# Second block's query, key, gate and pool columns by seven block products instead of eight

## The chip, the cores and the metric

The kernel runs on one core of one Trainium2 chip. The metric is the device time of one execution in microseconds (us). Matrix products run on TensorE ("PE" in the profile; "PEld" is its weight load). VectorE ("DVE") and ScalarE ("ACT") do the elementwise work, GpSimd ("POOL") issues the accumulating transfers, SyncE ("SP") issues most of the others. Each engine works through its own list of instructions in order, and waits on semaphores for the others.

## The reference

One layer of a decoder for 2048 tokens of width 1024, in float32:

```python
h = rmsnorm(x, mix_norm_g)
proj = h @ w_in                                  # 1024 x 2560
q, k, v, g, u = split(proj, 512 columns each)
y_ret  = silu(g) * head_rmsnorm(retention(rope(q), rope(k), v))   # 4 heads of 128
y_pool = pool_mixer(u, pool_w) * pool_scale      # 4 groups of 128, windows 2, 4, 8, 16
x = x + concat(y_ret, y_pool) @ w_out
x = x + cross_attn(rmsnorm(x), rmsnorm(mem))     # 4 heads, 256 memory tokens
x = x + conv_glu_ffn(rmsnorm(x))                 # 1024 -> 2 x 2816 -> 1024, causal width-3 convolution
return rmsnorm(x)
```

The change is in `h @ w_in` for the second half of the tokens. Of its 20 groups of 128 columns, 16 are touched: four query, four key, four gate and four pool groups. The four value groups are not.

## The kernel before

**Tiling.** Tokens stand along the free dimension, features along the 128 partitions. The tokens are two blocks of 1024 (`T`), each of two halves of 512 (`SUB`); the 1024 features are eight groups `k` of 128. Every float32 operand is split into a high and a low part: `hi = round(x)` on ACT, `lo = x - hi` on DVE (`split`, or `high` and `low`). A product is three matmuls, high x high, high x low, low x high (`passes`, L241 to L243), each 128x128 by 128x512. The parts of weights go through three slots of the tile Q, raw weights through five slots of the tile R.

**The stage around the change**, for each block: `values` makes v (192 matmuls). `head_inputs` makes gate, query and key of one head by `unit`: one group of 128 columns, two PSUM banks (one for each 512 tokens), 48 matmuls over k, then `evac`. For query and key that is the rotary embedding straight from PSUM on DVE. `pool_group` does the same for a pool group, then window sums on DVE. `retention` of a head is a generator: `unit` advances it once per 12 matmuls (`next(behind[0])`), so that a head's attention runs beside the next head's projections. It works on two halves `a` and `c` of four chunks each. `scores` (L740, transposed keys L742), `states` (L751, then three chained steps on DVE), `values` (L764, L766), squares on ACT (L770), a reciprocal root of some 12 tiny DVE operations, `mixed` (transposes L779, gate, split). Block 1 starts with pool groups 3 and 2, then values, heads 0 to 3, pool groups 0 and 1, and then the output projection, which reads all eight results `mix[k]` as split tiles from `B`.

**Seven products already stand in the MLP.** There weights of two column groups are combined beforehand by transfers (`weight_sums`, L906: four copies from SP and four accumulating ones from POOL for each pair, spread over the first stages by `next(under[0])`), tiles are combined by `sums_of`, and `run` works through seven block products of 12 matmuls per pair (`Member`, `gathered`): products 0, 2, 4 and 6 pile up in one bank, 1 and 5 in a second, 3 has a third, and after each product `evac` copies or adds the bank's present content.

**Order.** The program's order gives priorities; a scheduler in the compiler then sets the order on each engine. What it chose is quoted below where it matters.

## Time and profile before

| | |
|---|---|
| median of 3 runs | 2475.38 us (2471.82 to 2476.74) |
| the profiled execution | 2470.94 us, its span 2469.2 us |
| PE busy | 2430.5 us, 98% of the span |
| DVE busy | 1706.8 us, 69% |
| ACT busy | 1219.9 us, 49% |
| POOL busy | 182.9 us, 7% |
| TensorE clock, mean | 0.996 |

Matmuls are pipelined and the profile models their ends: a record reads 0.39 us though the next matmul starts about 0.23 us later. How fast PE goes is therefore read from the count of matmuls in a window, not from its busy share. DVE's and ACT's records overlap a little as well. A wait is time in which an engine sat idle before an instruction, with the instruction that released it.

### The profile page before, as it was taken

What the parts mean: (1) busy time and instruction counts of PE and PEld (TensorE: products, weight loads), DVE (VectorE), ACT (ScalarE), POOL (GpSimd) and SP (SyncE); (2) the same over time, 40 slices, a digit from 0 to 9 for tenths busy, and PEclk for the clock granted to TensorE, in tenths of its full rate; (3) what the DMA queues carried; (4) which work ended last, traced back from release to release, by engine and by line L of the source; (5) the groups of instructions that cost most, each with busy time, mean ns of one, the idle gap of its engine ahead of it and who ended that gap; (6) DMA issues with size and microseconds to landing.
All of it is one profiled execution on the core that took longest, in us unless ns stands there. A gap on an engine that the chain in (4) does not pass through costs nothing.

```text
span 2469.2 us, 33010 instructions
## 1 busy us (share of the span) xinstructions
PE 2430.5 (98%) x11390; PEld 2032.3 (82%) x11390; DVE 1706.8 (69%) x2913; ACT 1219.9 (49%) x2170; POOL 182.9 (7%) x240
## 2 busy tenths in 40 slices
PE   6999999999999999999999999999999999999997
PEld 6888888888888888888888888888888888888886
DVE  8646576564636574575679776896767688867875
ACT  6333423443421223434655555665555577666663
POOL 1010121100021110000000100020000000000000
PEclk9999999999999999999999999999999999999998
DMA  9363889726676674366568655765457479768951
GB/s 321 91 167 116 233 198 246 230 49 196 189 189 154 152 160 147 111 223 223 156 205 275 208 182 156 229 211 174 154 158 217 135 228 309 238 189 281 345 169 68
DMA packets 257176, 474.27 MB, mean 192 GB/s; under 512 B 26864, under 2 KB 56176, under 8 KB 257008
## 3 DMA queue, kind: packets, MB, share of 16 engines
q1 hardware_dynamic: 212912, 409.23, 50.7%
q0 software_dynamic: 19584, 34.61, 9.2%
q10 hardware_dynamic: 24512, 28.32, 3.3%
q8 instruction: 89, 1.46, 0.2%
q14 instruction: 79, 0.65, 0.1%
HBM read 370.87 MB, written 170.39 MB: 219 GB/s over the span
## 4 chain that ended last, share of the span: by engine, by line
PE 95%; DVE 2%; DMA 1%; ACT 1%; issue 0%; POOLq 0%; POOL 0%; SPq 0%; ACTq 0%; DVEq 0%
PE mm L241 30%; PE mm L243 30%; PE mm L242 30%; PE aux L751 1%; PE aux L852 1%; PE aux L764 1%; PE aux L740 1%; PE aux L766 1%; PE aux L243 1%; PE aux L242 1%; PE aux L241 1%; PE aux L317 1%; DVE Z L216 0%; DMA R<-wo 0%; DMA Z<-xT 0%
## 5 line engine op out<-in xcount | busy, mean ns | idle before, releaser
L241 PE MATMUL mm<-G,Q 128*128 128x512 f32 (+1 forms) x1888 | 726.2, 385 | 17.2 <-ACT Q L233 11.3
L243 PE MATMUL mm<-G,Q 128*128 128x512 f32 (+1 forms) x1888 | 724.7, 385 | 4.6 <-DVE Q L216 4.4
L242 PE MATMUL mm<-G,Q 128*128 128x512 f32 (+1 forms) x1888 | 723.8, 384 | 0.0
L242 PE MATMUL mm<-G 128*128 128x512 f32 (+1 forms) x1380 | 530.0, 384 | 0.0
L241 PE MATMUL mm<-G 128*128 128x512 f32 (+1 forms) x1380 | 528.3, 385 | 0.4 <-ACT T L474 0.4
L243 PE MATMUL mm<-G 128*128 128x512 f32 (+1 forms) x1380 | 528.2, 385 | 0.0
L241 PEld LDWEIGHTS mm<-G,Q 128*128 128x128 f32 x1888 | 357.0, 189 | 85.8 <-ACT Q L233 11.9
L243 PEld LDWEIGHTS mm<-G,Q 128*128 128x128 f32 x1888 | 356.6, 189 | 73.7 <-DVE Q L216 5.7
L242 PEld LDWEIGHTS mm<-G,Q 128*128 128x128 f32 x1888 | 357.0, 189 | 67.9 <-DVE G L216 0.4
L241 PEld LDWEIGHTS mm<-G 128*128 128x128 f32 x1380 | 259.3, 188 | 51.9 <-ACT T L474 0.6
L242 PEld LDWEIGHTS mm<-G 128*128 128x128 f32 x1380 | 259.3, 188 | 51.4
L243 PEld LDWEIGHTS mm<-G 128*128 128x128 f32 x1380 | 259.3, 188 | 51.3
L1008 ACT ACTIVATE G<-R 128x512 fp32r<-128x512 f32 (+1 forms) x272 | 167.2, 616 | 251.9 <-PE mm L242 243.4
L216 DVE TENSOR_TENSOR Q<-R,Q 128x512 fp32r<-128x512 f32 x235 | 162.5, 694 | 151.3 <-ACT Q L233 136.8
L216 DVE TENSOR_TENSOR Z<-Z,mm 128x512 f32<-128x512 f32 x284 | 193.9, 683 | 101.8 <-PE mm L243 101.6
L225 DVE SCALAR_TENSOR_TENSOR Z<-Z,vecs 128x1024 f32<-128x1024 f32 x176 | 224.7, 1281 | 50.4 <-ACT Z L1071 45.8
L216 DVE TENSOR_TENSOR G<-R,G 128x512 fp32r<-128x512 f32 (+1 forms) x268 | 178.6, 675 | 109.7 <-ACT G L1008 70.7
L233 ACT ACTIVATE Q<-R 128x512 fp32r<-128x512 f32 x150 | 93.6, 628 | 243.1 <-PE mm L242 221.4
L1008 ACT ACTIVATE Q<-R 128x512 fp32r<-128x512 f32 (+1 forms) x204 | 125.5, 615 | 98.0 <-PE mm L242 80.6
L216 DVE TENSOR_TENSOR G<-T,G 128x512 fp32r<-128x512 f32 (+1 forms) x201 | 133.0, 677 | 45.0 <-ACT G L957 31.0
L216 DVE TENSOR_TENSOR T<-T 128x512 f32<-128x512 f32 (+3 forms) x218 | 149.3, 689 | 18.0 <-ACT T L357 9.7
L1071 ACT ACTIVATE Z<-Z,vecs 128x1024 f32<-128x1024 f32 x88 | 109.1, 1241 | 33.0 <-DVE Z L216 32.1
(216 smaller groups left out, 2480.9 us busy)
## 6 DMA issues: line engine op xcount, KB each, us to landing
R<-Ud SPq DMA_DIRECT2D x176, 256.0 KB, 2.8
T<-Gd SPq DMA_DIRECT2D x168, 256.0 KB, 4.4
R<-w_up SPq DMA_DIRECT2D x132, 256.0 KB, 3.2
Gd<-Z SPq DMA_DIRECT2D x110, 256.0 KB, 2.8
Ud<-w_up SPq DMA_DIRECT2D x88, 256.0 KB, 6.3
R<-w_qkgu SPq DMA_DIRECT2D x32, 512.0 KB, 4.5
R<-Dd SPq DMA_DIRECT2D x64, 256.0 KB, 4.4
Gd<-T SPq DMA_DIRECT2D x56, 256.0 KB, 3.5
```

The costliest lines, as they stand in the source:

```text
L216: return eng.tensor_tensor(out=out, in0=a, in1=b, op=op)
L225: dve.scalar_tensor_tensor(out=out, in0=a, scalar=s, in1=b, op0=op0, op1=op1)
L233: act.activation(hi, src, AF.Copy)
L241: pe.matmul(ps, lh, rh, start=start, stop=False, skip_group_check=more)
L242: pe.matmul(ps, lh, rl, start=False, stop=False, skip_group_check=more)
L243: latest[0] = pe.matmul(ps, ll, rh, start=False, stop=stop, skip_group_check=more)
L317: pe.matmul(ps[:, t : t + 1], ap, one, start=True, stop=more is None)
L740: pe.matmul(col(sc, c), self.ch(k, c), self.ch(q, c), start=True, stop=True)
L751: pe.matmul(col(self.kv, c), col(self.kn.f, c), self.ch(v, c, h * T), start=True, stop=True)
L764: pe.matmul(col(y, c), col(self.pr.f, c), self.ch(v, c, h * T), start=True, stop=self.cur[c] is None)
L1008: act.activation(p2[:, 0, :w], self.raw[i].f[:, :w], AF.Copy)
L1071: act.activation(self.c[g].f, a[:, 2:], AF.Identity, bias=cb[:, f : f + 1], scale=cw[2][:, f : f + 1])
```

## The change

For block 1 alone, the 16 groups of 128 columns become eight pairs, worked through in the order of `PAIRS`. Numbers 0 to 3 are queries, 4 to 7 keys, 8 to 11 gates, 12 to 15 pool groups. A pair is a 2x2 block product (two column groups, two halves of the features, two halves of the tokens) done by seven products of 12 matmuls.

- The weights' sums go to `Ad` in DRAM by eight more jobs of `weight_sums`, ahead of the MLP's. `quarter_sums` reads x of the block again (16 transfers) and makes the token side's sums; three of the seven operands are new tiles (t1, t2, t3), the others stand in X.
- `values` now comes first, its weights loaded during the last unit of block 0's attention.
- `head_projections` runs 56 products. `evac` copies or adds, and `final` scales a finished quarter. A query's or key's rotary embedding takes two half copies on ACT into one shared scratch (`side`) and three DVE operations.
- Retention leaves its result unsplit (`out` is None) and scales y on ACT, four instructions a half, in place of one on DVE. Pool groups are summed in steps beside the products (`pool_steps`). The results are split only when the last pair is under way or done (`settle`), since t1 to t3 occupy their places until then. Pool group 0's result goes to the tile E, which is free only when head 3's result is split.
- Places: `B` is 12 slots of G and four of E, raw weights get 3 + 2 slots of R and S, the split weights five places during the stage.

```diff
+PAIRS = ((15, 8), (0, 4), (14, 9), (1, 5), (10, 11), (2, 6), (3, 7), (12, 13))
...
-    def values(rn, wp):
+    def values(rn, wp, step=lambda: None):
...
+                    step()
...
-                tt(dve, four(self.kn.f[:, :SUB]), four(y), bcast(rr, P), ALU.mult)
+                if out is not None:
+                    tt(dve, four(self.kn.f[:, :SUB]), four(y), bcast(rr, P), ALU.mult)
+                else:
+                    for c in range(4):
+                        act.activation(col(self.kn.f, c), col(y, c), AF.Identity, scale=rr[:, c : c + 1])
...
-        jobs = [((w_up[f], w_up[f + NF]), 0, 4, Ud[f]) for f in range(NF)]
+        jobs = [((w_qkgu[a], w_qkgu[c]), 0, 4, Ad[p]) for p, (a, c) in enumerate(PAIRS)]
+        jobs += [((w_up[f], w_up[f + NF]), 0, 4, Ud[f]) for f in range(NF)]
...
+    def quarter_sums(b, t1, t2, z3, z4):
+        for j in range(KT // 2):
+            x = [TT.take() for _ in range(4)]
+            for i, r in enumerate(x):
+                k, at = j + 4 * (i // 2), b * T + i % 2 * SUB
+                sp.dma_start(r.f[:, :SUB], xT[k * P : (k + 1) * P, at : at + SUB])
...
+            act.activation(t, x12, AF.Identity, scale=g1)
+            tt(dve, x12, x11, x12, ALU.subtract)
+            split(x12, *fourth(t1, j), g1)
...
+            stt(d3, x22, g2, t, ALU.mult, ALU.subtract)
+            stt(x11, x11, g1, d3, ALU.mult, ALU.add)
+            negated(x11, *fourth(t2, j))
...
+            stt(d4, x21, g2, x11, ALU.mult, ALU.subtract)
...
+    def head_projections(b, v, rb, tabs, t1, t2, z3, z4):
...
+            def evac(self, i, ps):
+                role, q = ((0, 0), (1, 1), (0, 1), (0, 0), (1, 1), (0, 1), (1, 0))[i]
+                d = self.acc[role][q]
+                if (role, q) == (1, 0):
+                    self.final(role, q, d, ps)
+                elif (role, q) in self.seen:
+                    tt(dve, d, d, ps, ALU.subtract if role else ALU.add)
+                    self.final(role, q, d, d)
+                else:
+                    self.seen.add((role, q))
+                    act.activation(d, ps, AF.Copy, scale=-1.0 if role else 1.0)
...
+                if kind < 2:
+                    cs, cols = tables[0], slice(q * SUB, (q + 1) * SUB)
+                    c, sn = cs.f[:, cols], cs.f[:, T + q * SUB : T + (q + 1) * SUB]
+                    for to, at in ((slice(0, 64), slice(64, 128)), (slice(64, 128), slice(0, 64))):
+                        act.activation(side[to], src[at], AF.Copy, scale=1.0 if src is d else -1.0)
+                    tt(dve, side, side, sn, ALU.mult)
+                    times(d, src, c)
+                    tt(dve, d, d, side, ALU.add)
...
+        items = [(m, i) for m in members for i in (range(7) if m is members[0] else (0, 2, 4, 6, 1, 3, 5))]
...
+        for at, (m, i) in enumerate(items):
...
+            for j in range(KT // 2):
+                passes(ps, [pr[:, h, j * P : (j + 1) * P] for h in range(2)], operand(i, j), j == 0 and i in (0, 1, 3), j == KT // 2 - 1, i != 3)
+            made[at].free()
+            m.evac(i, ps)
+            fill()
+            next(behind[0], None)
+            step()
+            step()
+            next(under[0], None)
+            if m is members[-1]:
+                if i in (1, 2, 4):
+                    (t1, t2, t3)[(1, 2, 4).index(i)].free()
+                if at >= len(items) - 6:
+                    settle()
+                    settle()
+            if at % 7 == 6 and m.groups[0] < 4:
+                finish()
+                behind[0] = kept(m.groups[0])
...
+        finish()
+        while todo:
+            step()
+        while ready:
+            settle(True)
...
+            v = values(lambda: normed[0], wv, between)
...
+            mix, S = head_projections(b, v, rb, tabs, t1, t2, z3, z4)
...
+            if n == KT - 1 and b + 1 < NB:
+                finish()
+                wv = []
+                behind[0] = opening(prob[0][0], wv)
```

In the rows below, `mm_...` is a PSUM bank of products and `aux_...` one of retention's. First PE at the end of the stage. Before, the second half of head 3 has its values (L766, L764) here, and its transposes (L779) stand further down:

```order
L766 MATMUL aux_6895<-T,Z_4498 128x128
L764 MATMUL aux_6895<-Z_4498,T 128x128
L766 MATMUL aux_6895<-T,Z_4498 128x128
L241 MATMUL mm_6874<-G,Q 128x512
L242 MATMUL mm_6874<-G,Q 128x512
L243 MATMUL mm_6874<-G,Q 128x512
```

Then, 51 matmuls after those values, in the output projection, PE has before:

```order
L243 MATMUL mm_7079<-G,Q 128x512
L779 MATMUL aux_6956<-consts,T 128x128 x4
L241 MATMUL mm_7079<-G,Q 128x512
L242 MATMUL mm_7079<-G,Q 128x512
L243 MATMUL mm_7079<-G,Q 128x512
```

Of the changed kernel, PE at the same place; the values are L790 and L792, the transposes L809, first for the first half (`aux_7037`), then for the second (`aux_7124`):

```order
L792 MATMUL aux_7043<-T,E_5473 128x128
L790 MATMUL aux_7043<-Z_4501,T 128x128
L792 MATMUL aux_7043<-T,E_5473 128x128
L809 MATMUL aux_7037<-consts,T 128x128 x4
L267 MATMUL mm_7166<-G,Q 128x512
L267 MATMUL mm_7240<-G,Q 128x512
L268 MATMUL mm_7166<-G,Q 128x512
L269 MATMUL mm_7166<-G,Q 128x512
L268 MATMUL mm_7240<-G,Q 128x512
L269 MATMUL mm_7240<-G,Q 128x512
L267 MATMUL mm_7167<-G,Q 128x512
L809 MATMUL aux_7124<-consts,T 128x128 x3
```

Between the second half's values and its transposes stand seven matmuls, where there were 51.

Second, PE where a bank is written on. Before, a unit fills its two banks in turn, and PE passes from one to the other:

```order
L242 MATMUL mm_5701<-G,Q 128x512
L243 MATMUL mm_5701<-G,Q 128x512
L241 MATMUL mm_5702<-G,Q 128x512
L242 MATMUL mm_5702<-G,Q 128x512
L243 MATMUL mm_5702<-G,Q 128x512
```

In the changed kernel, PE in the pair of query 0 and key 0, at the end of product 4 and the start of product 6:

```order
L268 MATMUL mm_5655<-G,S_5474 128x512
L269 MATMUL mm_5655<-G,S_5474 128x512
L267 MATMUL mm_5806<-G,S_5474 128x512
L268 MATMUL mm_5806<-G,S_5474 128x512
L267 MATMUL mm_5655<-G,Q 128x512
L268 MATMUL mm_5655<-G,Q 128x512
```

Product 6 adds to the bank that ACT has to copy after product 4, with two matmuls between; pairs (1, 5) and (2, 6) have the same distance, elsewhere it is five matmuls or more.

Third, DVE at a query's rotary embedding. Before, it reads the bank:

```order
L216 TENSOR_TENSOR Z_4498<-mm_5701,Z_4498 128x512
L216 TENSOR_TENSOR T<-mm_5701,Z_4498 64x512 x2
L216 TENSOR_TENSOR Z_4498<-Z_4498,T 128x512
L216 TENSOR_TENSOR Z_4498<-mm_5702,Z_4498 128x512
L216 TENSOR_TENSOR T<-mm_5702,Z_4498 64x512 x2
```

In the changed kernel, DVE in the pair of query 0 and key 0:

```order
L242 TENSOR_TENSOR Z_4501<-Z_4501,mm_5740 128x512
L242 TENSOR_TENSOR R<-R,Z_4501 128x512
L242 TENSOR_TENSOR Z_4501<-Z_4501 128x512
L242 TENSOR_TENSOR S_5474<-R,S_5474 128x512
L242 TENSOR_TENSOR Z_4501<-Z_4501,R 128x512
L242 TENSOR_TENSOR Q<-R,Q 128x512
L242 TENSOR_TENSOR R<-R,Z_4501 128x512
```

The second row works on the scratch that ACT has to fill after the first row; the fourth and sixth are the low parts of weights for products still to come, and stand behind it.

More of the change, by code (lines that the diff above doesn't have):

```diff
@@ L93, in free, with __init__, take @@
             assert self.first + j not in self.arena.freed
-            self.arena.freed[self.first + j] = self.arena.clock
-            self.arena.clock += 1
+            self.arena.freed[self.first + j] = Arena.tick()
         if self.back is not None:
             self.back()
+class Joined:
+    def __init__(self, *arenas):
+        self.arenas = list(arenas)
+    def take(self, n=1):
+        fits = [(a.oldest(n), at) for at, a in enumerate(self.arenas) if a.oldest(n) is not None]
+        assert fits, "no room"
+        return self.arenas[min(fits)[1]].take(n)
 class Places:
@@ L827, in attention @@
         scl, nscl = (smp.tile([P, 8], F32, tag="scl", name=nm("scl"), bufs=2) for _ in range(2))
-        room = B.take(2 * KT)
-        third = [Region(B, room.first + KT * i, KT) for i in range(2)] + [new_z(F32R).take(KT)]
-        prob = [third[1], third[0]]
+        low, high, far = B.arenas[0].take(KT), B.arenas[0].take(KT // 2), B.arenas[1].take(KT // 2)
+        tables = [low, None, new_z(F32R).take(KT)]
+        prob = [([high, far], [high.r, far.r]), ([low], [low.r[:, : 4 * T], low.r[:, 4 * T :]])]
         def load_m(hp):
@@ L1532, in trunk, with between @@
     for b in range(NB):
-        early = (3, 2) if b else ()
-        pooled = {g: pool_group(b, g, normed[1]) for g in early}
-        finish()
-        rn, rb, last = normed
-        assert rn is not None and rb
-        if b:
+        if b == 0:
+            rn, rb, last = normed
+            v = values(lambda: rn, wv)
+            with tc.issue_after(last.ins):
+                tabs = list(rope_tables(0))[-1]
+            cs = rope_scale(tabs, rb)
+            per = [(0, 1, 1), (0, 1, 1), (0, 2, 2), (0, 2, 3)]
+            mix = []
+            for h in range(HEADS):
+                qkg = head_inputs(h, rb, cs, lambda i: folded(per[h][i]))
+                mix.append(B.take(2))
+                behind[0] = retention(b, h, qkg, v, mix[h])
+            folded(100)
+            pooled = {g: pool_group(b, g, rb) for g in (0, 3, 2, 1)}
+            finish()
+            cs.free()
+            mix += [pooled[g] for g in range(4)]
+            mix = [(u, [u.r[:, :T], u.r[:, T:]]) for u in mix]
+        else:
+            t1, t2 = (B.arenas[0].take(4) for _ in range(2))
+            z3, z4 = Z.take(2), Z.take(2)
+            more_sums = quarter_sums(b, t1, t2, z3, z4)
+            def between():
+                next(behind[0], None)
+                if next(more_sums, None) is None:
+                    next(under[0], None)
+            v = values(lambda: normed[0], wv, between)
+            for _ in more_sums:
+                pass
+            finish()
+            rb = normed[1]
             tabs = [TT.take() for _ in range(2)]
@@ L1596, in trunk, with opening @@
         acc = []
+        def opening(room, wv):
+            yield
+            for r in room:
+                r.free()
+            for kp in range(KT // 2):
+                wv.append(value_weights(kp))
+                if kp:
+                    yield
         def fetch_acc(n):
```

271 lines of the change are left out of this document (217 added, 54 removed).

## The prediction

> **What bounds the kernel now.** I read the chain that ended last first, then PE's waits over the whole program, then the same waits in the stage of the change (640 to 960 us, block 1 from its first projections into the output projection), then busy time by windows: the stage, and two stretches of the MLP, which already works by seven products. First from the page:
>
> ```profile
> PE 95%; DVE 2%; DMA 1%; ACT 1%; issue 0%; POOLq 0%; POOL 0%; SPq 0%; ACTq 0%; DVEq 0%
> ```
>
> PE's waits of the whole program, the two largest:
>
> ```profile
> PE mm L241 <- ACT Q L233: 11.3, 4, 9.1
> PE mm L241 <- DVE T L216: 4.7, 1, 4.7
> ```
>
> And all that PE waits for from 640 to 960 us:
>
> ```profile
> PE mm L241 <- ACT G L233: 0.9, 1, 0.9
> ```
>
> PE carries the end, and in this stage it waits 0.9 us in all. So a matmul removed here is time removed, as long as no new wait comes; and any new wait is time added.
>
> ```profile
> core 0: us, PE busy (x) PEld busy (x) DVE busy (x) ACT busy (x) POOL busy (x), PEclk, DMA share, GB/s
> 658.00:912.00 254.00, 254.00 (x1295) 215.88 (x1294) 154.66 (x351) 56.57 (x140) 50.42 (x62) 1.00 0.72 168
> ...
> 1300.00:1350.00 50.00, 50.00 (x223) 41.40 (x222) 47.08 (x64) 28.19 (x43) 4.26 (x6) 1.00 0.83 280
> 1350.00:1400.00 50.00, 50.00 (x222) 41.44 (x221) 38.39 (x49) 28.52 (x43) 5.59 (x6) 1.00 0.68 214
> ```
>
> The stage takes 254 us, DVE is busy 61% of it, ACT 22%. A saturated PE runs 222 matmuls in 50 us: 0.2252 us each. In the first MLP window DVE is busy 94% and PE still runs 223; a full DVE alone does not stall PE.
>
> **What the change removes.** Eight pairs of 2x2 blocks take 8 x 7 x 12 = 672 matmuls in place of 8 x 8 x 12 = 768. Retention's and the later stages' matmuls keep their numbers. 96 x 0.2252 = **21.6 us less** of PE.
>
> **What it adds, and where it hides.** Counted over both orders, DVE gets 88 more operations of 128x512 and 32 fewer of 64x512; ACT gets 69 more of 128x512, 32 of 64x512, 32 of 128x128; POOL 32 more accumulating transfers; SP 104 more transfers of 256 KB and 16 fewer of 512 KB.
>
> ```profile
> L216 DVE TENSOR_TENSOR T<-mm,Z 64x512 f32<-64x512 f32 x64 | 44.0, 688 | 1.1
> L216 DVE TENSOR_TENSOR Z<-mm,Z 128x512 f32<-128x512 f32 x32 | 22.0, 687 | 14.8 <-PE mm L243 14.6
> L1054 ACT ACTIVATE Z<-mm 128x512 f32<-128x512 f32 x176 | 102.2, 581 | 3.2 <-PE mm L243 2.7 <-DVE Z L225 0.5
> L920 POOL DMA_DIRECT2D Ud<-w_up x22 | 25.1, 1159 | 7.0 <-DMA Ud<-w_up 6.5 <-issue 0.2
> ```
>
> Half the partitions cost DVE as much as all, so it is 56 more operations at 0.687: 38.5 us, and DVE goes from 154.7 to 193.2 of the remaining 232 us, 83%. ACT: 101 x 0.58 + 32 x 0.28 (the 128x128 rows below) = 67.5 us, 56.6 to 124, 53%. Both stay under the 94% that the MLP window carries with no loss of PE: at nothing, so far as only totals count. POOL's 32 accumulations at 1.16 at most are 37 us on an engine busy for 7% of the span; they stand ahead of the MLP's sums on its queue and delay these, which aren't needed until hundreds of us later. SP's copies into the sums are spread over the first stages. In the stage, 56 weight transfers of 256 KB and 16 of x replace 16 of 512 KB: 10 MB more in 232 us, 43 GB/s on top of 168; the first MLP window moved 280 without a stall. If the cover by the earlier loads fails, the price is one transfer's wait at the start of the first pair, a few us; the values come first and give 192 matmuls, 43 us, of time for that. These edits go in at nothing: values first, weight sums, the reread of x, the loads.
>
> **The end of the stage.** Here the cover goes. Before, 51 matmuls (11.5 us) stand between head 3's last values and its transposes, and the whole output projection's first part runs beside the rest. Afterwards seven (1.6 us) do, and pool group 0's result cannot be written until head 3's result is split, since it goes to the tile E. The second half of head 3, before, on PE, ACT and DVE:
>
> ```profile
> 893.47 1.06 PE L740 MATMUL aux<-Z 128*128 128x128 f32 x8
> ...
> 899.71 0.71 ACT L746 ACTIVATE T<-aux,consts 128x512 f32<-128x512 f32 x1
> ...
> 904.66 1.05 PE L751 MATMUL aux<-Z,T 128*128 128x128 f32 x8
> ...
> 910.54 0.39 PE L766 MATMUL aux<-T,Z 128*128 128x128 f32 x2
> 910.97 0.28 ACT L770 ACTIVATE T<-aux 128x128 f32<-128x128 f32 x1 [1.93 <-PE aux L766]
> ...
> 912.15 0.23 DVE L222 TENSOR_SCALAR sm<-sm,consts 128x4 f32<-128x4 f32 x1 [0.21 <-ACT T L770]
> ...
> 916.84 0.69 DVE L216 TENSOR_TENSOR T<-aux,sm 128x512 f32<-128x512 f32 x1
> ...
> 922.38 0.60 PE L779 MATMUL aux<-consts,T 128*128 128x128 f32 x4
> 923.02 0.75 DVE L225 SCALAR_TENSOR_TENSOR T<-aux,vecs,T 128x512 f32<-128x512 f32 x1 [0.85 <-PE aux L779]
> 923.87 0.63 ACT L233 ACTIVATE G<-T 128x512 fp32r<-128x512 f32 x1 [0.15 <-DVE T L225]
> 924.53 0.69 DVE L216 TENSOR_TENSOR G<-T,G 128x512 fp32r<-128x512 f32 x1 [0.76 <-ACT G L233]
> ```
>
> From scores to the last low part it took 925.2 - 893.5 = 31.7 us, with PE busy on other products throughout. In the new order, PE has from these scores to the last matmul that reads pool group 0's result only 69 matmuls (15.5 us) and retention's small ones (1.05 or 0.6 a group as above, some 5.5 us): 21.1 us of work. I walk the chain, from 0 at the scores, with the rows' durations. The states and values of both halves, with DVE's pool rows between them in the new order, end at 18.4 (before: 17.5). Squares and root take 5.9 (910.93 to 916.84) and the pool and split rows among them on DVE 1.8: 26.1. Scale on ACT 0.7 and transposes 0.6: 27.5. DVE has 2.5 us of pool rows first and reaches the gate at 28.6; gate 0.75, high 0.63, low 0.69: 30.7. Pool group 0's two highs and last low: 1.95 more, 32.6. The three matmuls that read it: 33.3. Minus 21.1: **12.2 us of waits**, in pieces (1.6 at the states, 2.6 at the values, 2.1 and 4.5 at the two transposes, the rest at the E tile). Low end: the measured chain less the 4.85 us for which the scaled result waited for its turn on PE (917.53 to 922.38), 26.9 - 21.1 = 5.8. High end: 31.7 + 1.95 + 1.8 + 2.5 = 37.9, less 21.1, 16.8. I take 12.2, as the new order's own walk, near the middle.
>
> **A bank used again too soon.** Three times (pairs of heads 0, 1, 2) two matmuls stand between product 4 and product 6, which waits for ACT's copy of product 4's bank.
>
> ```profile
> 1210.20 0.39 PE L243 MATMUL mm<-G,Q 128*128 128x512 f32 x1
> ...
> 1210.63 0.69 DVE L216 TENSOR_TENSOR Z<-Z,mm 128x512 f32<-128x512 f32 x1 [1.43 <-PE mm L243]
> ```
>
> A bank's reader starts 0.43 us after the last matmul; with ACT's copy of 0.58, 1.01. The last matmul and the two between cover 3 x 0.225 = 0.68. So 0.35 each, plus about 0.25 for an ACT already at work: 0.6 x 3 = **1.8 us** (0 if PE is late anyway; 4.5 if a whole ACT operation and a half stand ahead).
>
> **Rotary embeddings through the scratch.** Each finished quarter of a query or key now goes ACT, ACT, DVE, and low parts of the next product's weights stand behind that on DVE. Ends: 0, by the 94% window above, 6 if each of the four pairs loses 1.5 (two ACT operations and a little). Nearer to the zero row: 0.6 a pair, **2.4 us**.
>
> **Sum.** -21.6 + 12.2 + 1.8 + 2.4 = -5.2. The profiled execution is 2470.94 (span 2469.2 and 1.7 around it), which is 4.4 under the median of 2475.38, 0.9 under the lowest run. On the profiled execution this gives 2465.7; on the median, which is what I forecast, **2470**. 0.2%, 5 us, is about what a measurement of this kernel can tell from no change; the forecast lies right on that edge.
>
> The terms' ends: best -21.6 + 5.8 = -15.8, worst -21.6 + 16.8 + 4.5 + 6 = +5.7.
>
> **Rivals.**
> *Slower: the scratch is one, and it makes the weights late.* There is one scratch for all 16 query and key results. DVE's fourth row in the quoted order stands behind a row that waits for two ACT copies. If at each result ACT takes 0.58 x 2 with nothing to hide it, DVE's low parts come 1.2 us late and PE, which has only one product's weights (2.7 us) ahead, waits: 16 x 1.2 = 19 us. -21.6 + 12.2 + 1.8 + 19 = +11.4: 2486.8. It makes the change a loss of more than 0.2% from (4.95 + 21.6 - 14.0) / 16 = 0.8 us a result. For it: one shared place, DVE at 83%. Against: ACT at 53%, and the MLP runs ACT copies and DVE low parts mixed with PE full. 0.27.
>
> *Faster: the tail finds cover.* The scheduler's order leaves the output projection's other groups to run, DVE's pool rows fall in gaps, and the rest costs nothing: 5.8 or a little less, -16: 2459. For it: the chain's waits in pieces each need DVE at its busiest. Against: only 21.1 us of PE work. 0.25.
>
> *The clock falls in the tail.* Here the trace has one case, after PE's wait of 4.71 us:
>
> ```profile
> 33.15 0.58 PE L241 MATMUL mm<-G,Q 128*128 128x256 f32 x1 [4.71 <-DVE T L216]
> ```
>
> ```profile
> 32.00:36.00 4.00, 2.85 (x13) 2.86 (x14) 4.00 (x9) 4.00 (x9) 0.00 (x0) 0.52 0.60 211
> 36.00:40.00 4.00, 4.00 (x25) 4.00 (x24) 4.00 (x8) 4.00 (x6) 0.00 (x0) 0.63 0.53 140
> ```
>
> The clock was 0.52 and 0.63 in the 8 us behind it. That costs 4 x 0.48 + 4 x 0.37 = 3.4 us, so 2473.4. It needs one wait of about that length; my walk's longest is 4.5, between which PE does seven matmuls and four transposes. [...] I give it 0.08, since the pieces may well be shorter than the walk has them.
>
> That the change doesn't do what it says is excluded by the count of matmuls in the order: 96 fewer.
>
> **How the numbers follow.** Forecast 0.40 (own range 2465 to 2476, by one half of each term's spread); slower rival 0.27; faster rival 0.25; clock 0.08. Faster by over 0.2%, under 2470.4: the faster rival and about half of the forecast's cases, 0.44. Within: the other half and most of the clock rival, 0.27. Slower, over 2480.3: the slow rival and a rest, 0.29. The range runs from 2458, the faster rival with a little less tail, to 2487, the slow one.
>
> **What the changed profile would show.** PE's records fall by 96 in number. From the values to the last pair, matmuls come at 222 in 50 us with waits under 5 us in all; waits on ACT's copies ahead of product 6 of three pairs, about 0.6 each. DVE busy 190 us of the stage, ACT 125. At the end PE waits 12 us, at the states, values and transposes of head 3 and at pool group 0's result. The clock stays at 1.00. Wrong would be: waits of PE for low parts of weights all along the query and key pairs (the slow rival), a tail under 6 us (the fast one), waits for transfers of weight sums or x at the start of the first pair, which I hold at nothing, or another stage of the program that moves by more than 2 us.

## The result, and the profile after

| | before | changed |
|---|---|---|
| median | 2475.44 us (2471.82 to 2477.82, 12 runs) | 2483.24 us (2478.89 to 2487.78, 12 runs) |
| the profiled execution | 2470.94 us | 2478.89 us |
| span | 2469.2 us | 2477.0 us |

The ratio is 1.0035, with a 95% interval of 1.0025 to 1.0045: slower by 8.7 us, where 5 us less was forecast. The profiled execution of the changed kernel is the fastest of its twelve (six of them lie within 3.2 us of it, the other six from 5.5 to 8.9 us above it), so its trace can show less than what the others pay.

The page of the changed kernel, busy times and the chain that ended last:

```profile
PE 2422.2 (98%) x11294; PEld 2018.0 (81%) x11294; DVE 1730.7 (70%) x2969; ACT 1283.2 (52%) x2303; POOL 206.9 (8%) x272
...
PE 88%; DMA 5%; DVE 4%; ACT 1%; issue 1%; SPq 0%; POOLq 0%; POOL 0%; ACTq 0%; DVEq 0%
```

The 96 matmuls are gone (11390 to 11294 records). But transfers, not there before by more than 1%, now hold 5% of the chain, and DVE 4%. Where, is read from windows: first the kernel before, then the changed one, in five stretches (columns as in the prediction: length, busy time of PE, PEld, DVE, ACT and POOL, granted clock, DMA share, GB/s).

```profile
500.00:560.00 60.00, 60.00 (x286) 49.59 (x285) 36.49 (x88) 28.75 (x66) 0.00 (x0) 1.00 0.14 39
600.00:660.00 60.00, 60.00 (x271) 49.80 (x269) 32.81 (x52) 26.40 (x46) 6.59 (x8) 1.00 0.74 199
660.00:890.00 230.00, 230.00 (x1154) 194.91 (x1154) 136.81 (x305) 50.55 (x117) 46.11 (x56) 1.00 0.71 166
890.00:960.00 70.00, 69.14 (x338) 57.62 (x337) 44.05 (x97) 22.40 (x50) 6.55 (x8) 1.00 0.66 177
1000.00:1150.00 150.00, 150.00 (x700) 124.09 (x699) 95.76 (x203) 58.76 (x134) 0.40 (x4) 1.00 0.56 198
```

```profile
500.00:560.00 60.00, 58.04 (x274) 47.51 (x273) 41.87 (x100) 29.31 (x68) 0.66 (x1) 1.00 0.14 40
600.00:660.00 60.00, 55.62 (x233) 45.02 (x232) 31.98 (x51) 23.95 (x42) 10.75 (x13) 0.94 0.87 230
660.00:890.00 230.00, 228.00 (x1135) 190.53 (x1134) 163.77 (x350) 113.41 (x239) 31.99 (x39) 1.00 0.72 190
890.00:960.00 70.00, 62.94 (x284) 49.42 (x284) 44.01 (x110) 26.86 (x65) 23.72 (x30) 0.93 1.07 268
1000.00:1150.00 150.00, 149.07 (x696) 123.35 (x695) 96.70 (x206) 59.41 (x137) 13.30 (x18) 1.00 0.82 254
```

A stretch loses what PE is idle, and of its length the share by which the clock is down. From 600 to 660 us that is 4.4 + 60 x 0.06 = 8.0 us against none; from 890 to 960, 7.1 + 70 x 0.07 = 12.0 against 0.9; within the pairs, 660 to 890, 2.0; and 2.0 and 0.9 in two stretches that the change doesn't touch. A matmul's modelled end (0.39 us after its start) runs past the next start, so this view misses the first part of each wait. Counted from start to start in the trace, against 0.227 us for a 128x512 matmul and 0.1 us for a small one, 600 to 660 us cost 7.9 us more than before, 890 to 960 us 12.9, 660 to 890 us 3.9, 500 to 560 us 2.2 and 1000 to 1150 us 0.9; the first 270 us cost 1.5 more. That is 29.3 of losses against 21.8 of saving, 7.5 of the 7.8 us by which the span is longer.

**The start of the second block.** PE's waits from 600 to 660 us in the changed kernel, and the chain there:

```profile
PE mm L267 <- ACT Q L259: 3.7, 1, 3.7
PE mm L269 <- DVE Q L242: 0.7, 1, 0.7
```

```profile
608.24 18.80 DMA T<-xT
627.06 0.73 ACT G L262
...
629.77 0.61 DVE Q L242
630.42 0.79 PE mm L269
```

A tile of x was 18.8 us on its way; ACT waited 14.0 us for it, with a weight's high part (L259), which PE needed, queued behind, and DVE waited for ACT:

```profile
627.06 0.72 ACT L262 ACTIVATE G<-T,vecs 128x512 fp32r<-128x512 f32 x1 [13.99 <-DMA T<-xT]
627.69 0.61 ACT L382 ACTIVATE T<-T 128x512 f32<-128x512 f32 x1
628.21 0.61 ACT L259 ACTIVATE Q<-R 128x512 fp32r<-128x512 f32 x1
```

PE was idle from 625.2 to 628.9 us, still in the stage before the values. Afterwards it ran at half its clock:

```profile
630.00:636.00 6.00, 5.58 (x13) 4.42 (x14) 5.08 (x9) 4.38 (x9) 1.63 (x2) 0.50 1.04 257
```

Why x was late, SyncE's transfers show, changed kernel first, then the kernel before (start, length, instruction):

```profile
588.67 3.08 SPq L950 DMA_DIRECT2D Ud<-w_up  x5
592.01 0.38 SPq L551 DMA_DIRECT2D T<-xT  x1
592.43 2.82 SPq L950 DMA_DIRECT2D Ud<-w_up  x3
595.45 0.64 SPq L551 DMA_DIRECT2D T<-xT  x1
596.14 7.31 SPq L950 DMA_DIRECT2D Ud<-w_up  x6
...
605.65 2.31 SPq L950 DMA_DIRECT2D Ud<-w_up  x2
608.24 3.87 SPq L551 DMA_DIRECT2D T<-xT  x2
```

```profile
596.92 2.44 SPq L917 DMA_DIRECT2D Ud<-w_up  x4
...
608.77 2.42 SPq L917 DMA_DIRECT2D Ud<-w_up  x4
```

Sixteen copies of the MLP's weight sums, with POOL's accumulations after them, go out from 588 to 608 us; before it was eight, spread behind two weight loads. The median time of a tile of x to its landing, 600 to 630 us, changed and before:

```profile
T<-xT SPq DMA_DIRECT2D x3, 256.0 KB, 17.3
```

```profile
T<-xT SPq DMA_DIRECT2D x5, 256.0 KB, 6.4
```

In these 30 us 15 transfers of sums were issued, where it had been 11. The bytes alone don't tell how full the DMA engines were: POOL's accumulating transfers moved 3.28 MB for 60.9% of their time, SP's transfers 4.20 MB for 42.5%, so a byte of POOL's queue took 1.8 times as long as one of SP's; how much of that is the accumulating itself is not shown. In all it was 271 GB/s with every slice of the window at 90% or more.

**The end of the stage.** PE's waits from 885 to 960 us in the changed kernel:

```profile
PE mm L267 <- ACT G L259: 3.0, 2, 1.5
PE aux L809 <- ACT T L804: 1.6, 1, 1.6
PE aux L777 <- ACT T L772: 1.4, 1, 1.4
```

They stand at retention's states (L777) and transposes (L809) and at the last results' high parts (L259). Around them the clock falls twice, for 6.8 us at 922.9 and for 3.4 us at 933.1:

```profile
915.00:920.00 5.00, 3.97 (x25) 3.17 (x25) 4.72 (x16) 1.45 (x4) 4.17 (x5) 1.00 1.08 267
920.00:925.00 5.00, 1.86 (x8) 0.94 (x6) 4.39 (x22) 2.84 (x13) 2.44 (x4) 0.79 1.06 225
925.00:930.00 5.00, 4.69 (x12) 2.90 (x13) 4.96 (x15) 1.71 (x6) 3.64 (x6) 0.53 1.06 162
930.00:933.00 3.00, 1.46 (x6) 0.68 (x5) 2.00 (x3) 0.90 (x2) 1.43 (x2) 1.00 1.13 172
933.00:937.00 4.00, 4.00 (x12) 3.12 (x12) 2.50 (x4) 1.92 (x4) 0.81 (x1) 0.57 1.07 212
```

### The profile page after: what moved, and what is told of

It is laid out like the page before. It is cut to its first block, busy times and chain, and to the rows that moved or that the text cites. A ratio compares the mean times of both kernels' runs of the same rounds, so it can differ in the third digit from the quotient of the medians.

```text
span 2477.0 us, 33287 instructions
## 1 busy us (share of the span) xinstructions
PE 2422.2 (98%) x11294; PEld 2018.0 (81%) x11294; DVE 1730.7 (70%) x2969; ACT 1283.2 (52%) x2303; POOL 206.9 (8%) x272
## 4 chain that ended last, share of the span: by engine, by line
PE 88%; DMA 5%; DVE 4%; ACT 1%; issue 1%; SPq 0%; POOLq 0%; POOL 0%; ACTq 0%; DVEq 0%
PE mm L267 28%; PE mm L269 28%; PE mm L268 27%; DMA T<-xT 1%; DVE T L242 1%; DMA T<-Xd 1%; DVE Z L242 1%; PE aux L342 1%; PE aux L268 1%; PE aux L267 1%; PE aux L269 1%; PE aux L777 0%; DVE Q L242 0%; DMA T<-pos 0%; DMA Hd<-T 0%
## 5 line engine op out<-in xcount | busy, mean ns | idle before, releaser
L267 PE MATMUL mm<-G,Q 128*128 128x512 f32 (+1 forms) x1720 | 663.2, 386 | 23.5 <-ACT Q L259 14.6
L269 PE MATMUL mm<-G,Q 128*128 128x512 f32 (+1 forms) x1720 | 660.8, 385 | 6.3 <-DVE Q L242 6.1
L268 PE MATMUL mm<-G,Q 128*128 128x512 f32 (+1 forms) x1592 | 609.8, 383 | 0.2 <-DVE G L242 0.2
L268 PE MATMUL mm<-G,E 128*128 128x512 f32 x1084 | 421.6, 389 | 0.0
L267 PE MATMUL mm<-G,E 128*128 128x512 f32 x1084 | 420.2, 390 | 0.0
L269 PE MATMUL mm<-G,E 128*128 128x512 f32 x1084 | 419.2, 389 | 0.0
L267 PEld LDWEIGHTS mm<-G,Q 128*128 128x128 f32 x1720 | 326.6, 190 | 88.9 <-ACT Q L259 15.9
L269 PEld LDWEIGHTS mm<-G,Q 128*128 128x128 f32 x1720 | 326.4, 190 | 70.7 <-DVE Q L242 8.4
L268 PEld LDWEIGHTS mm<-G,Q 128*128 128x128 f32 x1592 | 302.1, 190 | 57.3 <-DVE G L242 1.5
L242 DVE TENSOR_TENSOR Z<-Z,mm 128x512 f32<-128x512 f32 x296 | 201.4, 681 | 101.2 <-PE mm L269 101.0
L251 DVE SCALAR_TENSOR_TENSOR Z<-Z,vecs 128x1024 f32<-128x1024 f32 x176 | 224.5, 1279 | 50.0 <-ACT Z L1104 46.4
L267 PEld LDWEIGHTS mm<-G,E 128*128 128x128 f32 x1084 | 203.5, 188 | 42.4 <-ACT Z L1186 0.3
L269 PEld LDWEIGHTS mm<-G,E 128*128 128x128 f32 x1084 | 203.5, 188 | 42.3
L268 PEld LDWEIGHTS mm<-G,E 128*128 128x128 f32 x1084 | 203.5, 188 | 42.1
L1041 ACT ACTIVATE E<-R 128x512 fp32r<-128x512 f32 (+1 forms) x165 | 101.5, 615 | 142.8 <-PE mm L268 135.3
L242 DVE TENSOR_TENSOR T<-T 128x512 f32<-128x512 f32 (+3 forms) x224 | 152.9, 688 | 23.2 <-ACT T L382 11.1
L242 DVE TENSOR_TENSOR Q<-R,Q 128x512 fp32r<-128x512 f32 x153 | 106.1, 696 | 74.5 <-ACT Q L259 50.8
L242 DVE TENSOR_TENSOR G<-T,G 128x512 fp32r<-128x512 f32 (+1 forms) x181 | 119.0, 673 | 42.5 <-ACT G L990 30.5
L1041 ACT ACTIVATE Q<-R 128x512 fp32r<-128x512 f32 (+1 forms) x157 | 96.9, 618 | 99.6 <-PE mm L268 73.8
L990 ACT ACTIVATE G<-T 128x512 fp32r<-128x512 f32 x157 | 95.9, 625 | 54.5 <-DMA T<-Hd 27.3
L242 DVE TENSOR_TENSOR E<-R,E 128x512 fp32r<-128x512 f32 (+1 forms) x131 | 87.4, 671 | 51.2 <-ACT E L1041 42.3
```

The source lines that it names most:

```text
L242: return eng.tensor_tensor(out=out, in0=a, in1=b, op=op)
L251: dve.scalar_tensor_tensor(out=out, in0=a, scalar=s, in1=b, op0=op0, op1=op1)
L267: pe.matmul(ps, lh, rh, start=start, stop=False, skip_group_check=more)
L268: pe.matmul(ps, lh, rl, start=False, stop=False, skip_group_check=more)
L269: latest[0] = pe.matmul(ps, ll, rh, start=False, stop=stop, skip_group_check=more)
L990: act.activation(hi, x, AF.Copy)
```

## The experiments

Differences in us are differences of the ratios to the kernel before, times 2475. "Excess" is the time lost against full-rate matmuls, from start to start, in the one execution of each run that was profiled; it is good to some 0.2 us.

| run | ratio to before (95% interval) | excess 600:660 | excess 890:960 |
|---|---|---|---|
| before | 1 | -0.2 | 2.4 |
| changed | 1.0035 (1.0025, 1.0045) | 7.7 | 15.3 |
| no sums in the values | 0.9978 (0.9969, 0.9987) | -0.1 | 14.0 |
| sums paced by x's transfers | 1.0011 (1.0001, 1.0022) | -0.1 | 16.2 |
| before, with eight more jobs of sums | 1.0029 (1.0017, 1.0042) | -0.1 | 2.8 |
| more cover at the end | 1.0001 (0.9992, 1.0009) | 8.0 | 11.5 |
| no sums in the values, more cover | 1.0027 (1.0017, 1.0036) | -0.1 | 12.9 |
| two late results not read | 1.0026 (1.0016, 1.0036) | 8.2 | 15.0 |
| the same, no sums in the values | 1.0002 (0.9994, 1.0010) | -0.1 | 17.1 |
| eight of the MLP's jobs left out | 1.0021 (1.0012, 1.0030) | 7.7 | 13.7 |
| changed, none of the MLP's sums | 0.9977 (0.9969, 0.9986) | -0.1 | 14.3 |
| before, eight jobs of sums only | 0.9994 (0.9986, 1.0003) | -0.1 | 2.6 |
| none of the sums, three late results not read | 0.9956 (0.9944, 0.9968) | -0.1 | 7.9 |
| none of the sums, more cover | 0.9966 (0.9955, 0.9978) | -0.2 | 11.5 |
| no sums in the values, sums faster in the first block | 1.0048 (1.0035, 1.0061) | -0.1 | 15.6 |
| no sums in the values, more cover, no sums after the last weight | 1.0014 (1.0005, 1.0024) | -0.1 | 12.1 |
| no sums in the values, no sums after the last weight | 1.0000 (0.9991, 1.0009) | -0.2 | 14.3 |

### The sums inside the values

`between` was written so that a step of the sums comes when `more_sums` has ended. But a generator that goes on also yields None, so all 16 steps advance the sums; and a job waits for the weight load last noted (`issue_after(fetched[0])`), which `value_weights` does not renew. The last one noted was out at 588 us.

```diff
             def between():
                 next(behind[0], None)
-                if next(more_sums, None) is None:
-                    next(under[0], None)
+                next(more_sums, None)
```

> The changed kernel, but the 16 steps inside the second block's values no longer advance the MLP's weight sums; the jobs come later, beside the pairs. Theory 'burst': those steps release four jobs (16 copies, 16 accumulations) at once at 588 us, since no weight load renews their pacing; they hold up x's transfers (17 us to landing), ACT and DVE wait in order, PE waits 4.4 us and then runs at half clock for 6.8 us. Without them the excess of 600 to 660 us goes from 7.9 us to under 1, the half clock at 629 us is gone, and the time falls by about 7.5 us, to 2475.5 (ratio to before 1.000). Rival 'volume': the values-first order and the bytes added are to blame whatever the pacing; then the wait stays within 2 us of what it was, 2481 to 2483.

```profile
600.00:660.00 60.00, 60.00 (x267) 49.69 (x266) 39.64 (x62) 29.20 (x50) 0.00 (x0) 1.00 0.47 154
```

The wait and the half clock are gone, and the time falls by 14.1 us to 2469.19, 5.4 us below the kernel before (0.9978; 0.9969 to 0.9987). The mechanism holds; the size was nearly twice what the trace of the changed kernel showed. The two traces set the fastest of twelve executions against the second slowest of ten (2471.06), and these spans differ by 7.7 us, about what the wait and the half clock cost. Where the other 6 us of the medians lie no trace shows; that the late tile costs more in slower executions is a guess. This version is faster than both kernels, by 0.2% than the kernel before.

Pacing instead of removing:

```diff
-                sp.dma_start(r.f[:, :SUB], xT[k * P : (k + 1) * P, at : at + SUB])
+                fetched[0] = sp.dma_start(r.f[:, :SUB], xT[k * P : (k + 1) * P, at : at + SUB])
```

> The changed kernel, but each repeated transfer of x renews the pacing of the weight sums, so that those jobs start no sooner than these transfers. Burst: as in the run without those steps, 2475.5, the wait before 629 us under 1 us; the end of the stage may be a little better, since the jobs are not put off as far. Volume: 2481 to 2483, with the wait at another place.

```profile
700.00:750.00 50.00, 45.52 (x189) 35.87 (x188) 35.72 (x59) 20.15 (x35) 11.53 (x14) 0.97 0.89 209
```

The excess at the start is gone, but more than half of the gain is lost again: the wait moved to 700 to 750 us, 4.5 us idle and some half clock. The median, 2477.0, is 1.5 us above what was expected. In that stretch SP's queue has the sums between the repeated loads of x and the first pairs' weights.

Is it their number or their bunching? The sums of eight pairs are left out, and their products read other pairs' sums (the line for that is not shown):

```diff
-        jobs += [((w_up[f], w_up[f + NF]), 0, 4, Ud[f]) for f in range(NF)]
+        jobs += [((w_up[f], w_up[f + NF]), 0, 4, Ud[f]) for f in range(8, NF)]
```

> The changed kernel, with the sums of eight of the MLP's 22 pairs left out (their products read the sums of other pairs, which leaves the MLP's numbers wrong and its work the same), so that there are as many jobs of sums as in the kernel before. The burst of four jobs at 588 us is still there. Theory 'burst': it is the bunching, not the number of jobs, and the excess at 600 to 660 us stays at 6 to 8 us, the time within 3 us of the changed kernel, 2480 to 2484. Rival 'volume' (adding these jobs alone to the kernel before cost 6.6 us): 2476 to 2478.

With as many jobs as the kernel before, the excess at the start is unchanged (7.7). The 3.5 us gained are just beyond the 3 that "burst" allowed, with intervals that overlap. So at the start it is the bunching, not the number of jobs. The opposite run adds the eight jobs to the kernel before (their tile `Ad` and the list `pairs_` are not shown):

```diff
+        jobs = [((w_qkgu[a], w_qkgu[c]), 0, 4, Ad[p]) for p, (a, c) in enumerate(pairs_)]
-        jobs = [((w_up[f], w_up[f + NF]), 0, 4, Ud[f]) for f in range(NF)]
+        jobs += [((w_up[f], w_up[f + NF]), 0, 4, Ud[f]) for f in range(NF)]
```

> The kernel before, with the eight jobs of weight sums added ahead of the MLP's (their results are not read): the added traffic alone, without the new products. Burst: in the kernel before two jobs run beside x's transfers, paced by the pool groups' weight loads, so PE waits nowhere more than 1 us longer: 2475 to 2477. Volume: the jobs that now end up beside the tail and the loads cost what they cost in the changed kernel, +5 to +8 us: 2480 to 2483.

```profile
1000.00:1150.00 150.00, 144.69 (x673) 118.64 (x672) 94.98 (x202) 59.25 (x136) 20.11 (x26) 1.00 0.90 271
```

7 us slower, as "volume" said and "burst" did not. The profiled execution is one of its slowest, 2487.43, so its losses sum to more: 3 us in the first 270 us, 3 from 270 to 500, 2.3 from 500 to 560, 6 from 1000 to 1150, and nothing at 600 to 660. Around 500 us DVE waits 7.1 us for the rotary tables' positions, as in the changed kernel (below). From 1000 to 1100 us POOL is now busy with sums for 19.9 us, where it was idle, and from 1090 to 1130 us DVE waits 8.3 us for attention's loads, where it was 2.7. So the added traffic can cost this much alone, and where it costs depends on what it happens to meet. Taking nearly all sums away looks at it from the other side; only the eight new jobs are kept in the changed kernel, or eight of the MLP's in the kernel before, and the MLP's products read these (not shown):

```diff
-        for w, k0, n, to, in jobs:
+        for w, k0, n, to, in jobs[:8]:
```

> The changed kernel with the MLP's 34 jobs of weight sums left out, only the eight new ones kept (the MLP reads other sums of the same size, so its numbers are wrong and its work the same): no sums run beside the loads of x, the pairs and the end of the stage. Theory 'collisions': the start (7.9 us of excess at 600 to 660) and the transfer part of the end go; beside the kernel before with as few jobs, -21.8 of matmuls, 3 within the pairs and 8 to 12 for the chains at the end leave -7 to -11 us. Rival 'order': the waits come from the order of the work itself, and the two differ by 0 to +5 us.

> The kernel before, with eight jobs of weight sums and the MLP's others left out in the same way (the MLP's numbers are wrong, its work the same). It hardly waited for transfers: 2470 to 2475 by either theory; it is what the run above is to be compared with.

Without any of the MLP's sums the changed kernel takes 2469.01, as it does with all of them but none inside the values. The kernel before hardly gains (0.9994). The two differ by 0.0017, 4.2 us, less than the 7 to 11 expected. The end has 11.7 us of the loss, near the top of the 8 to 12 allowed for it:

```profile
890.00:960.00 70.00, 63.49 (x286) 50.41 (x285) 42.10 (x97) 25.67 (x63) 0.00 (x0) 0.93 0.34 109
```

DMA share 0.34 in place of 1.07, and nearly the same loss: the end of the stage is not a matter of transfers. With 3.8 within the pairs that would leave 6.3 us of gain; the other 2 us are not placed. Both profiled executions are the slowest of their run; in them the changed kernel loses 4.6 us more in the first 270 us.

Advancing the sums faster in the first block, with none in the values:

```diff
-    quarter, slow = [0], [True]
+    quarter, slow = [0], [False]
```

> No weight sums advanced inside the values, and in the first block's stage one step of sums per 12 matmuls in place of every second: the jobs are done earlier, where the DMA engines are busy for 20 to 60% of the time, and fewer are left for the end of the second block's stage. Theory 'collisions': 2464 to 2468, below the 2469.2 without this. Rival: the sums meet the first block's loads instead, 2471 or more.

2485.42 (1.0048; 1.0035 to 1.0061): as the rival said, 2471 or more.

```profile
500.00:560.00 60.00, 55.13 (x253) 45.03 (x252) 36.09 (x84) 22.22 (x54) 2.54 (x3) 0.97 0.28 68
```

Against the run without sums in the values the excess grew by 4.4 at 270 to 480 us, by 4.5 at 500 to 560 and by 5.5 at 750 to 800. A low DMA share over a stretch didn't mean that there was room. At 500 us it is the late tile again, now the positions for the rotary tables, for which DVE waits in order (waits of DVE, 470 to 530 us, this run and then the changed kernel):

```profile
DVE T L246 <- DMA T<-pos: 13.3, 1, 13.3
```

```profile
DVE T L246 <- DMA T<-pos: 7.6, 1, 7.6
```

In the kernel before it is shorter:

```profile
DVE T L220 <- DMA T<-pos: 2.9, 1, 2.9
```

### The end of the stage

More cover for it: S as two more places for split weights, and the second output unit in the first one's order (the last two lines are pieces of one long line).

```diff
-        spare = new_s(F32)
-        raws = Places([(R, j * T) for j in range(3)] + [(spare, j * T) for j in range(2)], T)
-        prs = Places([(Q, j * T) for j in range(3)], T)
+        spare = new_s(F32R)
+        raws = Places([(R, j * T) for j in range(3)], T)
+        prs = Places([(Q, j * T) for j in range(3)] + [(spare, j * T) for j in range(2)], T)
...
-(7, 6, 0, 1, 2, 5, 3, 4) if n == 0
+(7, 6, 0, 1, 2, 5, 3, 4) if n < 2
```

> The changed kernel, with S as two more places for split weights in the output projection (raw weights get three) and its second unit in the order of the first, so that 18 more matmuls can run before head 3's and pool group 0's results are read. Theory 'no cover': the 12.9 us of excess from 890 to 960 us are the chain of head 3, and 18 matmuls (4.1 us) take their length off the waits and most of the half clock (5.1 us) with it: excess 4 to 6 us, time about 2475.5. Rival 'transfers': the DMA engines are full there (share 1.08) and the waits are for them; then the excess stays within 2 us of 12.9, and the time at 2482 to 2484.

The time is 8.4 us less, as expected, but the excess at the end fell by 3.8 only, to 11.5 where 4 to 6 was expected, and 2.0 lie at 500 to 560 us; where the rest of the gain comes from was not found. With no sums to disturb it, the same edit gives 2.7 us by the ratios, less than the 4 to 8 expected and with intervals that overlap:

> The changed kernel without the MLP's 34 jobs of sums (which leaves the MLP's numbers wrong and its work the same), with the two more places for split weights: what the added cover at the end is worth where no transfers of sums can disturb it. Theory 'no cover': 4 to 8 us less than the 2469.0 without it, 2461 to 2465. If the gain of the run with this edit alone was chance of how the transfers fell, 2468 to 2470.

Its excess at the end is 11.5 against 14.3, so the cover is worth about 3, not 8.

Who waits for what there? The first two output units read other results in place of the late ones (pieces of one long line).

```diff
-for r in mix[k][1]]
+for r in mix[k - 3 if b and n < 2 and k in (3, 4) else k][1]]
```

> The changed kernel, in which the first two units of the second block's output projection read head 0's and head 1's results in place of head 3's and pool group 0's, so that nothing waits for the end of head 3 there (this leaves out two of the eight parts of the sum in two of eight units; the work is the same). Theory 'chain': the excess from 890 to 960 us, 15.3 against 2.4 before, falls to about 3, and the time by 12 us, to 2471. Rival 'transfers': the weights and x arrive late there, and the excess stays at 10 or more: 2480 to 2483.

2.2 us less in place of 12, with intervals that overlap, and the excess stayed at 15.0. This looks like the rival "transfers", but PE's longest wait there was for pool group 1's high part; head 3 and pool group 0 were only two of three late results.

```profile
927.99 0.80 PE L267 MATMUL mm<-G,Q 128*128 128x512 f32 x1 [5.04 <-ACT G L259]
```

With pool group 1 replaced as well, and without the sums:

```diff
-k in (3, 4)
+k in (3, 4, 5)
```

> The changed kernel without the MLP's sums, in which besides the first two output units of the second block read heads 0, 1 and 2 in place of head 3 and pool groups 0 and 1, the three results that are finished last (with only head 3 and pool group 0 replaced, PE waited 5.0 us for pool group 1). Theory 'three late results': the excess from 890 to 960 us falls to 3 to 5, and the time by 6 to 9 us against the run without sums. Rival 'retention in PE's queue': PE stops at head 3's own values and transposes, whoever reads them; then it falls by less than 3.

```profile
890.00:960.00 70.00, 65.86 (x312) 53.98 (x311) 45.76 (x104) 27.12 (x63) 0.00 (x0) 0.95 0.39 125
```

The excess falls from 14.3 to 7.9 and the time by 5.2 us, between what the two theories said: of the 11.7 us that the end loses, the three results make a good half. Of what is left, PE waits 2.5 us at head 3's transposes, which stand in its queue whoever reads them, and 1.5 us for a late high part, and the clock is at half for 6.8 us. The wait moves between them as one is taken away. Replacing two of the three, with no sums in the values, was expected at 2458:

> The same, with no weight sums advanced inside the values as well: neither the start's nor the end's wait. If these two are what the forecast missed or priced, the time is before's less the 21.6 us of matmuls, plus the waits within the pairs (3 us) and some 2 us spread elsewhere: 2474.9 - 21.6 + 5 = 2458. If other costs of the added transfers matter, it stays above 2463.

It took 2475.80 us, 6 us more than without sums in the values alone; DVE waited 8.7 us at the end for the residual's x, and the excess there grew to 17.1.

### The two gains together

> Both edits that paid: no weight sums advanced inside the values, and two more places for split weights with the second output unit in the order of the first. If the two costs are separate (the start 14 us, the end 8 us off the changed kernel's median), 2483.2 - 14 - 8 = 2461 us, ratio to before 0.9945. If the end's gain in the run before came from the transfers that moved with it, not from the cover, nothing is added: 2468 to 2470.

2482.32, where 2461 was expected: 12 us slower than the first edit alone. The chain from 870 to 900 us:

```profile
866.81 8.80 DMA Ud<-w_up
875.68 9.69 DMA R<-wout_r
...
887.63 0.79 PE mm L267
```

Twelve copies of sums went out ahead of the output projection's first weights, and ACT, then PE (5.5 us, and half the clock after it: 0.43 us from matmul to matmul until 892.5 us, 0.23 from there) waited. To tell a stale pacing from the fewer raw places:

```diff
-            next(under[0], None)
+            if fetches:
+                next(under[0], None)
```

> No weight sums advanced inside the values, the two more places for split weights, and sums advanced beside the pairs only while weights of the pairs are still to be fetched, so that none is released by a load long past. Theory 'stale pacing': the 5.5 us wait and the half clock at 887 us of the run with both edits, where twelve copies of sums stood ahead of the output projection's first weights, are gone: 2463 to 2468. Rival 'three raw places': the wait comes from having three places for raw weights in place of five and stays, 2472 or more.

> The same without the two more places for split weights (five places for raw weights). Stale pacing: within 2 us of the run with no sums in the values, 2467 to 2471, since that run lost nothing to it at the end. If the sums put off collide later, 2473 or more.

```profile
850.00:890.00 40.00, 39.32 (x219) 33.73 (x218) 32.16 (x76) 25.39 (x60) 9.00 (x11) 1.00 0.86 218
```

The wait is gone with three raw places kept, so it was the bunch. But 2476.46 (1.0014) is not 2463 to 2468: the jobs put off cost 3 us of excess from 1000 to 1100 us and 7 from 1150 to 1300, where the MLP starts. With five raw places it is 2471.14 (1.0000), 5 us more than without this edit, and between what "stale pacing" (2471 at most) and its rival (2473 or more) said.

## Why the forecast was wrong

**The step that failed: "These edits go in at nothing: values first, weight sums, the reread of x, the loads."** It cost 7.9 us in the profiled execution, and leaving out the sums in the values is worth 14 on the median. The forecast set averages against each other, 43 GB/s more on 168 where 280 had run without a stall. But it took only one late tile, since ACT and DVE work in order (neither ran anything in the 14.0 us before the tile; then ACT took L262, L382 and L259 from 627.1 us on, and DVE L251 and L242 from 627.8 on); and bytes were the wrong measure, since the DMA engines were full at 271 GB/s from 600 to 630 us (share 1.09; it was 0.83 where 280 had run), where 3.28 of the 8.14 MB were POOL's accumulations. The forecast held the sums' copies to be "spread over the first stages". SP's rows above have 16 of them between x's loads, where there had been eight, each four behind a weight load; the orders that the forecast quotes are PE's and DVE's. Leaving those steps out removes the wait, the half clock and 14 us: this is shown; where 6 of the 14 lie is open. The fallback in the same step, "one transfer's wait at the start of the first pair, a few us", had the place wrong, since the wait came before the values, and left out what a late tile does to everything queued behind it.

The terms by themselves:

- **21.6 us saved.** Right: 96 records fewer, 0.227 us from start to start, 21.8.
- **End of the stage, 12.2 (6 to 17).** 12.9 measured. That the size came out is luck, for its make-up did not. The waits were 6.9 us, not 12.2: 1.4 at the states, 0.3 at the values, 1.6 at the transposes and 3.0 at the late results' high parts, where the walk had 1.6, 2.6, 6.6 and 1.4, and 0.6 at two others. Up to 5 us are half clock (10.2 us of it), which the forecast kept out of the sum. The walk also has no wait for pool group 1's result, for which PE stood 5.0 us once the other two were not read.
- **Bank reuse 1.8 and scratch 2.4.** 3.9 more excess from 660 to 890 us, against 4.2; this too is the sum and not the terms. Waits for ACT's copies (L1608) are 0.2 there, not 1.8. The other waits are three of 0.5 us for a weight's high part on ACT (L1041) and one of 0.2 at the states; what the rest of the 3.9 is was not found. The slower rival, the scratch that makes weights late, didn't happen: it needed 0.8 us at each of 16 results. The stage from 658 to 890 us had DVE busy for 165.8 us and ACT for 114.8, where 193 and 124 were worked out.
- **The clock.** It was said to need one wait of about 4.7 us, from a single case (4.71 us of waiting at 33 us of the kernel before), and given 0.08. The runs do not bear that out. It fell three times in the stretches that the change touches. At 629 us it followed 3.7 us of waiting. At 923 us the longest wait had been 1.6 us; in the 8 us before, PE waited 1.4, 0.2, 0.2 and 1.6 us, and over the ten us before 925 it was busy for 5.8. At 933 us the fall followed a wait of 1.5 us. Which pattern of waits brings it about is not shown.
- **Elsewhere, nothing.** About 4.6 us in four places whose products the change doesn't touch (0.9 and 0.6 in the first 270 us, 2.2 around 530, 0.9 around 1100). The weight sums are shifted by eight jobs in all of them; adding these jobs to the kernel before cost 7 us. Around 500 us DVE waits 4.7 us longer for the positions, and the kernel before with the added jobs does so too (7.1 us, and 2.3 us of excess): there the jobs alone are enough. The run with more cover, with as many jobs, loses only 0.2 there, so it isn't the same in every execution. At the other places it was not settled which transfer met which load.

The sum of what the forecast had terms for was -21.8 + 12.9 + 3.9 = -5.0, against its -5.2. The start's 7.9 and the 4.6 elsewhere, both held at nothing, turn it to +7.5, and the profiled spans differ by 7.8. On the median, leaving the sums out of the values turns the sign back, to 5.4 us faster than before.

How the packets of x's late tile were mixed with those of the sums no run here shows; x's tiles took 17.3 us to land beside 15 transfers of sums and 6.4 us beside 11.

## What to carry to other kernels

Before work is put "beside" other work at no cost, read the queue that carries it, row by row, at the places where an engine that works in order waits for a load: a bunch in front of one late tile cost here what the averages of bandwidth did not tell. A pacing that hangs on the last load goes stale where the loads change hands, so check what renews it. And where several results are late together, taking one off the path shows the next; price the group, not the last one.

## What the runs showed of the hardware

TensorE's clock fell to half for 6.8 us after no wait longer than 1.6 us (at 923 us); at half clock, where it read 0.50 and a 128x512 matmul started 0.43 us after the one before in place of 0.23, 6.8 us are worth 3.4 us of matmuls less, where PE has work for all of it. In the run with both edits the clock also fell after a wait of 5.5 us (0.43 us from matmul to matmul there too). From 600 to 630 us of the changed kernel, a byte on POOL's queue, whose transfers accumulate, took 1.8 times the DMA engines' time of a byte on SP's queue (3.28 MB for 60.9% of it, 4.20 MB for 42.5%). The changed kernel's executions range over 9 us and those without sums in the values over 4; but those of the run with both edits, which has no late tile at 629 us, range over 9 too, so what spreads them is not shown.
